# Attention heads on the whole array: zero-padded low query parts and meta tokens in place of 64- and 16-row products

## The chip, the cores and the metric

The kernel runs on one core of one Trainium2 chip. The metric is the device time of one execution in microseconds (us). TensorE multiplies (PE in the profile, its weight loads are PEld), VectorE (DVE), ScalarE (ACT) and GpSimd (POOL) do the elementwise work, and SyncE (SP) issues most DMAs. Each engine takes its own instructions in the order in which they were put into the program.

## The reference: what is computed

A trunk of two layers over 16 learned meta tokens and 512 input tokens (T = 528) of 1024 features. Layer 0 is a forgetting attention with 16 heads of 64 features, layer 1 a gated DeltaNet with 8 heads of 128; each is followed by a feed-forward part with a causal convolution. The change is in the attention alone, which is, for one head:

```python
q, k = rmsnorm(q, q_gain), rmsnorm(k, k_gain)
c = cumsum(log_sigmoid(fl + b_forget))
s = q @ k.T * 64 ** -0.5 + c[:, None] - c[None, :]
p = softmax(where(causal, s, -1e30))
o = (p @ v) * sigmoid(og)
```

All inputs and outputs are float32.

## The kernel before

**Tiling and stages.** Features lie on the partitions, tokens on the free axis. The tokens are worked on in two halves: A with 272 (16 meta tokens and 256 others) and B with 256. Weights come as units of 1024 input features by 128 output features. `dense` (L300 to L317) makes one unit's product for one half: eight feature tiles, and for each three matmuls at L312, since every float32 operand is split into a high and a low float32r part (high times high, high times low, low times high), so 24 matmuls of 128 x 128 weights over 256 or 272 columns. `push` (L425) runs half A of a unit at once and half B four units later.

**The attention stage** has 33 input units: one for the forget gates, then for each of eight pairs of heads (loop at L531) one for queries, keys, values and output gates. A pair's heads are e = 0 and e = 1, with 64 features each, so that a pair fills the 128 partitions.

- `qk` (L545 to L579) norms queries and keys. For keys it writes one tile `KS` per head: the high parts on that head's 64 partitions, the low parts on the other 64. For queries it writes per head a tile `QS` with the high parts on both halves of the partitions, and one tile `QL` for both heads, with the low parts of head e on head e's 64 partitions.
- `vproj` (L581 to L607) turns the values so that tokens lie on the partitions, and splits them: `VV` holds four blocks of 128 tokens, `VM` the 16 meta tokens on 16 partitions for each head (0 to 15 and 32 to 47).
- `attend` (L609 to L708) runs when a half's output gates are through `dense`. Its query blocks are `QB` (L490): block 0 is the 16 meta tokens, blocks 1 to 4 have 128 tokens. Half A takes blocks 0, 1 and 2, half B 3 and 4. `scores` (L624) makes for each head and block the product `QS` by `KS` (128 rows, L637), the product `QL` by the high keys on 64 rows (L638), and adds the causal mask as a bf16 product (L640); block 4 has its keys in two segments. DVE adds the decays (L641), ACT exponentiates (L644), DVE normalizes (L645, L646).
- `flip` (L651) transposes the probabilities on PE, a 128 x 128 block of keys at a time (L671), and splits them into `PTH` (ACT, L674) and `PTL` (DVE, L675). The first 32 keys, with the meta tokens, are transposed apart, 32 wide: those of head 0 to partitions 0 to 31 (L662), those of head 1 by a plain matmul with the identity to partitions 32 to 63 (L663, two passes). They become `PMH` and `PML` (L664, L665).
- `values` (L678) makes for each head and half the product of probabilities and values at L694: high and low probabilities over two (A) or four (B) blocks of 128 tokens, and for the meta tokens a product over 16 rows with `PMH` and one with `PML`.

**What sets the order.** The kernel is emitted unit by unit, and the framework puts each engine's instructions in an order at build time, by priorities and a simulated timeline (`schedule_with_timeline_sim=True`, L1470). So the heads' products lie between the `dense` products of the following units in PE's queue. The steps of `qk`, `vproj` and `og` behind `dense` have a raised priority (`tc.high_priority(offset=400)`).

**PSUM.** A tile is one bank. In the attention (L126) `dense` has two banks, `sc` (scores) two, `pt` (transposes) two, `av` and `pn` one each. `flip` takes one `pt` bank for block 0, two for blocks 1 to 3 and three for block 4; `vproj` takes one for each half.

**Weights.** ACT makes each unit's high part (L285), and for nearly all attention units GpSimd makes the low part in two instructions (L292). GpSimd also writes half of `QS` (L574), zeroes 16 columns of block 0's scores (L648) and does a step of the gates (L720).

Of the kernel before, what the change touches and what calls it, by code (L numbers as in the profile page):

```python
# [28 lines left out]
# estimated times (us) after which the DeltaNet's tasks go on  # L29
# [8 lines left out]
# order of the DeltaNet's units: queries, keys, values, output gates (H) and output projection, of head pairs  # L38
# [5 lines left out]
# units of the DeltaNet that leave work to GpSimd: low parts of weights, convolution taps, silu products  # L44
# [60 lines left out]
def trunk(ctx, tc, h0, wflat, params, out):  # L105
# [5 lines left out]
    # token range of the halves; the last layer leaves out the meta tokens but the two that its convolution sees  # L111
# [10 lines left out]
    # PSUM: one bank per tile; which ring of banks a kind of tile takes depends on the phase  # L122
# [48 lines left out]
    # constants  # L171
# [82 lines left out]
        # runs the tasks on, past their times, until a condition holds  # L254
# [15 lines left out]
    # weight stream  # L270
# [60 lines left out]
    # (mean of squares + eps) ** -0.5 per token, spread over the partitions in PSUM;  # L331
    # half A is covered by three chunks of 128 tokens, the last two of which overlap;
    # GpSimd adds the squares of the tiles
# [39 lines left out]
    # h * gain split in two float32r parts; the per-token factor is applied after the product  # L373
# [48 lines left out]
    # the job pipeline: half B of a unit runs LAG units behind half A  # L422
# [26 lines left out]
    # ---------------- output projections into m, then post-norm and next pre-norm  # L449
# [28 lines left out]
    # ---------------- FoX attention  # L478
# [13 lines left out]
    def attention_heads(layer, OH, OL, cx):  # L492
# [4 lines left out]

        def evac_f(u, half):
# [11 lines left out]
            # log_sigmoid(z) = min(z, 0) - log1p(exp(-|z|))  # L510
# [20 lines left out]
        for m in range(8):  # L531
            H = {}

            def head_tiles(m=m, H=H):
                if H:
                    return
                for e in range(2):
                    H["k", e] = ap.tile([P, T], F32R, name="KS", tag="KS", bufs=4)
                # values in two parts, [high, low] of head 0 and [low, high] of head 1
                H["v"] = ap.tile([P, 4, 2, 2, DH], F32R, name="VV", tag="VV", bufs=2)  # L540
                H["vm"] = ap.tile([48, 2, DH], F32R, name="VM", tag="VM", bufs=2)
                for half in range(2):
                    H["sg", half] = ap.tile([P, 272], F32, name="SG", tag="SG", bufs=4)

            def qk(u, half, which, H=H, m=m, head_tiles=head_tiles):  # L545
# [4 lines left out]
                with tc.high_priority(offset=400):  # L550
# [5 lines left out]
                    sx = ap.tile([P, 2, 272], F32R, name="SX", tag="SX", bufs=2)[:, :, :n]  # L556
                    nc.scalar.copy(sx[:, 0], sq)
                    nc.vector.tensor_tensor(sx[:, 1], sq, sx[:, 0].bitcast(F32), op=ALU.subtract)
                    nc.tensor.matmul(pn[:, :n], blk[:], sx[:, 0], start=True, stop=False)
                    nc.tensor.matmul(pn[:, :n], blk[:], sx[:, 1], start=False, stop=True)  # L560
                    # (mean of squares + eps) ** -0.5
# [3 lines left out]
                    if which == "q":  # L565
                        for e in range(2):
                            H["q", half, e] = ap.tile([P, 272], F32R, name="QS", tag="QS", bufs=4)
                        H["ql", half] = ap.tile([P, 272], F32R, name="QL", tag="QL", bufs=2)
                    for e in range(2):
                        a, b = (slice(0, 64), slice(64, 128)) if e == 0 else (slice(64, 128), slice(0, 64))  # L570
                        if which == "q":
                            S, L = H["q", half, e][:, :n], H["ql", half][:, :n]
# [8 lines left out]
            def vproj(u, half, H=H, m=m):  # L581
# [3 lines left out]
                with tc.high_priority(offset=400):  # L585
# [7 lines left out]
                    if half == 0:  # L593
                        nc.tensor.transpose(pt[:NM, 256:384], vr[:, 0:NM], ident[:])
                    b0 = blocks[0] - 1
                    VV, VM = H["v"], H["vm"]
                    sv = pt[:, 0:256].rearrange("p (k e x) -> p k e x", k=2, e=2)
                    for e in range(2):
                        vh, vl = VV[:, b0:b0 + 2, e, e, :], VV[:, b0:b0 + 2, e, 1 - e, :]
                        nc.scalar.copy(vh, sv[:, :, e, :])  # L600
                        nc.vector.tensor_tensor(vl, sv[:, :, e, :], vh.bitcast(F32), op=ALU.subtract)
                    if half == 0:
                        for e in range(2):
                            sv = pt[:NM, 256 + DH * e:256 + DH * e + DH]
                            o = slice(32 * e, 32 * e + NM)
                            nc.scalar.copy(VM[o, e, :], sv)
                            nc.vector.tensor_tensor(VM[o, 1 - e, :], sv, VM[o, e, :].bitcast(F32), op=ALU.subtract)  # L607

            def attend(half, H=H, m=m):  # L609
# [5 lines left out]
                PMH = ap.tile([64, 272], F32R, name="PMH", tag="PMH", bufs=2)  # L615
                PML = ap.tile([64, 272], F32R, name="PML", tag="PML", bufs=2)
# [7 lines left out]
                def scores(e, qb):  # L624
                    a = slice(0, 64) if e == 0 else slice(64, 128)
                    cB = Z[e][0]
                    QS, QL, KS = H["q", half, e], H["ql", half], H["k", e]
                    qs, ql = QB[qb]
                    ke = qs + ql
                    S = ap.tile([P, T], F32, name="S", tag="S", bufs=4)  # L630
                    st = ap.tile([P, 4], F32, name="st", tag="st", bufs=6)
                    segs = ((0, ke),) if ke <= 512 else ((0, 264), (264, 264))
                    for i, (k0, kn) in enumerate(segs):
                        sc = psum_tile("sc")
                        lastseg = k0 + kn == ke
                        o = sc[:ql, 0:kn]
                        nc.tensor.matmul(o, QS[:, qs - s:ke - s], KS[:, k0:k0 + kn], start=True, stop=False)  # L637
                        nc.tensor.matmul(o, QL[a, qs - s:ke - s], KS[a, k0:k0 + kn], start=False, stop=not lastseg)  # L638
                        if lastseg:
                            nc.tensor.matmul(sc[:ql, kn - ql:kn], identb[:ql, :ql], cmask[:ql, :ql], start=False, stop=True)  # L640
                        nc.vector.tensor_tensor_reduce(out=S[:ql, k0:k0 + kn], in0=o, in1=cB[:ql, k0:k0 + kn], scale=1.0, scalar=3e38, op0=ALU.add, op1=ALU.min, accum_out=st[:ql, i:i + 1])  # L641
                    if len(segs) == 2:
                        nc.vector.tensor_tensor(st[:ql, 0:1], st[:ql, 0:1], st[:ql, 1:2], op=ALU.min)
                    nc.scalar.activation(S[:ql, 0:ke], S[:ql, 0:ke], AF.Exp, scale=-1.0, bias=st[:ql, 0:1], accum_out=st[:ql, 2:3])  # L644
                    nc.vector.reciprocal(st[:ql, 3:4], st[:ql, 2:3])  # L645
                    nc.vector.tensor_scalar(S[:ql, 0:ke], S[:ql, 0:ke], st[:ql, 3:4], None, op0=ALU.mult)  # L646
                    if qb == 0:
                        nc.gpsimd.memset(S[:ql, 16:32], 0.0)  # L648
                    return S

                def flip(qb, SS):  # L651
                    qs, ql = QB[qb]
                    ke = qs + ql
# [821 lines left out]
```

## Time and profile before

| what | value |
|---|---|
| median of 3 runs | 1652.77 us (1651.1 to 1657.88) |
| span of the profiled execution | 1652.0 us |
| PE, PEld busy | 96%, 91% of the span |
| DVE, ACT, POOL busy | 68%, 49%, 30% |
| mean granted clock of TensorE | 0.978 |
| moved from and to HBM | 131.54 and 5.36 MB, 83 GB/s |

The profiled execution has no other time than its span, first to last instruction; it lies 0.8 us under the median of the runs. The input units of the attention run from about 5 us to about 393 us; then come its output projection and the first feed-forward part (to about 810 us), the DeltaNet (to about 1230 us) and the second feed-forward part. A matmul's duration in the profile (293 ns for a 128 x 256 one at L312) is longer than its share of PE's time, since matmuls overlap; the distance from one start to the next tells what a matmul costs, and the timeline shows that.

### The profile page before, as it was taken

Reading aid. Unit: us, or ns where it says so; the run is one execution under the profiler, and the core shown is the slowest. Engines: PE = TensorE matmul, PEld = TensorE weight load, DVE = VectorE, ACT = ScalarE, POOL = GpSimd, SP = SyncE. Lnnn points to the kernel's source line nnn. Section 1 sums busy time; section 2 is a strip of 40 time slices with the busy share of each in tenths; the row PEclk is TensorE's granted clock in tenths of the full one; section 3 lists DMA queues with packets and bytes.
Section 4 is the critical chain, followed back from the end, with each engine's and each line's share of the span. In section 5 each row is a group of like instructions: output and inputs, shape, how many; then the busy total and the mean of one; then the engine's idle time right before and its main releaser. Section 6 shows DMA issues by size and latency. Waiting matters only on the chain.

```text
span 1652.0 us, 33460 instructions
## 1 busy us (share of the span) xinstructions
PE 1588.7 (96%) x12702; PEld 1505.8 (91%) x12702; DVE 1128.9 (68%) x2652; ACT 817.3 (49%) x1949; POOL 490.5 (30%) x979
## 2 busy tenths in 40 slices
PE   8999999999999999999989899999997999999996
PEld 7888888888999999999978888898997999999996
DVE  7777777774897467566588765576559874675764
ACT  7666666663564344244455455545555543443441
POOL 6333333211530000001354763836235210100012
PEclk9999999999999999999989998989998999999998
DMA  5222222231222322322223323131232223323221
GB/s 169 85 72 66 58 66 72 72 117 59 83 90 81 95 94 81 99 90 90 81 84 100 91 70 75 44 98 44 63 117 84 90 84 96 103 79 101 90 78 52
DMA packets 63328, 139.05 MB, mean 84 GB/s; under 512 B 18584, under 2 KB 31288, under 8 KB 62784
## 3 DMA queue, kind: packets, MB, share of 16 engines
q1 hardware_dynamic: 62544, 134.55, 27.5%
q8 instruction: 100, 1.64, 0.4%
q0 software_dynamic: 480, 2.15, 0.4%
q14 instruction: 60, 0.49, 0.1%
q10 hardware_dynamic: 144, 0.22, 0.0%
HBM read 131.54 MB, written 5.36 MB: 83 GB/s over the span
## 4 chain that ended last, share of the span: by engine, by line
PE 76%; DVE 8%; POOL 7%; DMA 3%; ACT 2%; issue 2%; SPq 1%; POOLq 0%; DVEq 0%; ACTq 0%
PE ps L312 64%; PE av L694 3%; POOL PR L1172 3%; POOL RB L1173 3%; PE sc L638 2%; DVE cv L759 1%; DVE h L412 1%; DVE bt L411 1%; PE pt L671 1%; DMA w<-wflat 1%; PE sc L637 1%; DVE wl L292 1%; DMA AB<-dA 1%; DVE xl L378 1%; PE pt L663 1%
## 5 line engine op out<-in xcount | busy, mean ns | idle before, releaser
L312 PE MATMUL ps<-xh,wh 128*128 128x256 f32 (+4 forms) x2464 | 716.2, 293 | 19.1 <-DVE ub L743 10.9
L312 PE MATMUL ps<-xl,wh 128*128 128x256 f32 (+4 forms) x2464 | 710.9, 289 | 2.8 <-DVE xl L378 2.8
L312 PE MATMUL ps<-xh,wl 128*128 128x256 f32 (+4 forms) x2464 | 709.5, 289 | 0.0
L312 PEld LDWEIGHTS ps<-xh,wh 128*128 128x128 f32 (+1 forms) x2464 | 468.1, 191 | 28.2 <-DVE ub L743 8.1
L312 PEld LDWEIGHTS ps<-xl,wh 128*128 128x128 f32 (+1 forms) x2464 | 470.0, 191 | 7.0 <-DVE xl L378 3.9
L312 PEld LDWEIGHTS ps<-xh,wl 128*128 128x128 f32 (+1 forms) x2464 | 469.8, 191 | 1.3 <-issue 0.3
L285 ACT CAST wh<-w 128x1024 fp32r<-128x1024 f32 (+3 forms) x226 | 224.7, 996 | 190.3 <-PE ps L312 168.8
L292 DVE TENSOR_TENSOR wl<-w,wh 128x1024 fp32r<-128x1024 f32 (+4 forms) x191 | 221.7, 1161 | 101.1 <-ACT wh L285 100.5
L759 DVE SCALAR_TENSOR_TENSOR cv<-ub,prm,cv 128x256 f32<-128x256 f32 (+2 forms) x494 | 243.8, 498 | 40.7 <-ACT cv L750 31.6
L312 PE MATMUL ps<-ah,wl 128*128 128x256 f32 (+2 forms) x704 | 199.5, 284 | 0.0
L312 PE MATMUL ps<-ah,wh 128*128 128x256 f32 (+2 forms) x704 | 199.3, 283 | 0.0
L312 PE MATMUL ps<-al,wh 128*128 128x256 f32 (+2 forms) x704 | 199.1, 283 | 0.0
L750 ACT ACTIVATE cv<-ub,prm 128x256 f32<-128x256 f32 (+2 forms) x224 | 113.5, 509 | 144.8 <-DVE ub L743 144.6
L743 DVE TENSOR_TENSOR ub<-ps,r 128x256 f32<-128x256 f32 (+2 forms) x224 | 95.1, 427 | 93.9 <-PE ps L312 91.1
L312 PEld LDWEIGHTS ps<-ah,wh 128*128 128x128 f32 x704 | 132.7, 189 | 0.0
L312 PEld LDWEIGHTS ps<-al,wh 128*128 128x128 f32 x704 | 132.5, 188 | 0.0
L312 PEld LDWEIGHTS ps<-ah,wl 128*128 128x128 f32 x704 | 132.4, 188 | 0.0
L353 POOL TENSOR_TENSOR ssq<-ssq,sq 128x256 f32<-128x256 f32 (+2 forms) x98 | 89.3, 914 | 139.8 <-ACT sq L352 138.1
L292 POOL TENSOR_TENSOR wl<-w,wh 128x512 fp32r<-128x512 f32 x70 | 95.1, 1379 | 110.9 <-ACT wh L285 104.5
L746 POOL COPY cy<-ub 128x2 f32<-128x2 f32 (+1 forms) x112 | 38.5, 346 | 276.0 <-DVE ub L743 275.7
L742 POOL COPY ub<-cy 128x2 f32<-128x2 f32 (+1 forms) x112 | 32.1, 286 | 199.5 <-DVE cv L759 164.2
L1172 POOL TENSOR_TENSOR PR<-RB,AB 128x60 f32<-128x60 f32 (+24 forms) x124 | 50.6, 408 | 24.3 <-DMA AB<-dA 9.9
(310 smaller groups left out, 2481.6 us busy)
## 6 DMA issues: line engine op xcount, KB each, us to landing
w<-wflat SPq DMA_DIRECT2D x176, 512.0 KB, 3.6
w<-wflat SPq DMA_DIRECT2D x32, 448.0 KB, 3.3
cB<-cdram SPq DMA_DIRECT2D x16, 264.0 KB, 3.3
w<-wflat SPq DMA_DIRECT2D x16, 256.0 KB, 2.7
h<-h SPq DMA_DIRECT2D x8, 272.0 KB, 4.4
cB<-cdram SPq DMA_DIRECT2D x16, 136.0 KB, 3.1
h<-h SPq DMA_DIRECT2D x8, 256.0 KB, 5.6
AB<-dA SPq DMA_DIRECT2D x16, 128.0 KB, 2.8
```

Of the source, the lines that this page charges most:

```text
L285: nc.scalar.copy(wh[:], w32)
L292: eng.tensor_tensor(wl[:, c], w32[:, c], wh[:, c].bitcast(F32), op=ALU.subtract)
L312: tok(nc.tensor.matmul(o, w[:, a], r[:, c0:c1], start=(i == 0), stop=(i == tot - 1)))
L353: nc.gpsimd.tensor_tensor(self.acc[:, :n], self.acc[:, :n], sq[:, :n], op=ALU.add)
L638: nc.tensor.matmul(o, QL[a, qs - s:ke - s], KS[a, k0:k0 + kn], start=False, stop=not lastseg)
L694: nc.tensor.matmul(o, l, r, start=(i == 0), stop=(i == len(mm) - 1))
L743: nc.vector.tensor_tensor(ub[:, c0:c0 + n], ps, r[:, :n], op=ALU.mult)
L746: nc.gpsimd.tensor_copy(c[:, :c0], ub[:, n:n + c0])
L750: nc.scalar.activation(cv, ub[:, c0:c0 + n], AF.Identity, scale=w[c0])
L759: nc.vector.scalar_tensor_tensor(cv, ub[:, i:i + n], w[i], cv, op0=ALU.mult, op1=ALU.add)
L1172: nc.gpsimd.tensor_tensor(t, R3[:, 0:a, l:l + 1].to_broadcast([P, a, w]), A3[:, l:l + 1, l + 1:32].to_broadcast([P, a, w]), op=ALU.mult)
L1173: nc.gpsimd.tensor_tensor(R3[:, 0:a, l + 1:32], R3[:, 0:a, l + 1:32], t, op=ALU.subtract)
```

## The change

Every product of the heads gets 128 rows and 128 columns of weights:

- `QL` becomes one tile per head, with zeros on the other head's 64 partitions, so that L638's product runs over 128 rows. The tiles (`QZ`, two for each head) are made once, zeroed by GpSimd at the start of the stage, and taken in turn.
- Block 0's scores are made for 128 query rows, of which 16 are used; the mask product has 128 x 128 weights. GpSimd zeroes 112 columns of the scores on 128 partitions in place of 16 on 16.
- The first keys' probabilities are transposed as 128 x 128 blocks, one for each head, both by a transpose. One tile `PM` (again two, zeroed once) holds the high parts of the 16 meta rows on partitions 0 to 15 and their low parts on 32 to 47, zeros elsewhere, for both heads side by side on the free axis.
- The meta tokens' values become a fifth block of `VV`: GpSimd copies the first 32 tokens four times side by side, and one 128 x 128 transpose puts them on the partitions, so that rows 0 to 15 and 32 to 47 both hold the meta tokens. One product of 128 rows takes the place of the two of 16 rows in `values`.
- `vproj` splits the values with fewer, wider instructions: one on ACT and one on DVE for both heads, and one each for the meta block.
- `flip` takes the bank of the meta rows first: one bank for block 0, two for block 1 and three for blocks 2, 3 and 4.
- `SX` becomes `SH` (two buffers) and `SL` (one), and the gates' tile `SG` has two buffers in place of four and is taken in `og`.

The diff without the parts that only drop comments:

```diff
+        zt = bl[:, 0:1]
+        nc.vector.memset(zt, 0.0)
+        QZ = [[ap.tile([P, 272], F32R, name=f"QZ{i}{e}") for e in range(2)] for i in range(2)]
+        PZ = [ap.tile([P, 2, 272], F32R, name=f"PZ{i}") for i in range(2)]
+        for i in range(2):
+            for e in range(2):
+                b = slice(64, 128) if e == 0 else slice(0, 64)
+                nc.gpsimd.tensor_copy(QZ[i][e][b, :], zt[b, :].to_broadcast([64, 272]))
+            nc.gpsimd.tensor_copy(PZ[i][:], zt.unsqueeze(1).to_broadcast([P, 2, 272]))
+        ring = {"q": 0, "p": 0}
+
+        def persistent(name, tiles):
+            ring[name] += 1
+            return tiles[ring[name] % 2]
...
-                H["v"] = ap.tile([P, 4, 2, 2, DH], F32R, name="VV", tag="VV", bufs=2)
-                H["vm"] = ap.tile([48, 2, DH], F32R, name="VM", tag="VM", bufs=2)
-                for half in range(2):
-                    H["sg", half] = ap.tile([P, 272], F32, name="SG", tag="SG", bufs=4)
+                H["v"] = ap.tile([P, 5, 4, DH], F32R, name="VV", tag="VV", bufs=2)
...
-                    sx = ap.tile([P, 2, 272], F32R, name="SX", tag="SX", bufs=2)[:, :, :n]
+                    sh = ap.tile([P, 272], F32R, name="SH", tag="SH", bufs=2)[:, :n]
+                    sl = ap.tile([P, 272], F32R, name="SL", tag="SL", bufs=1)[:, :n]
...
-                        H["ql", half] = ap.tile([P, 272], F32R, name="QL", tag="QL", bufs=2)
+                        H["ql", half] = persistent("q", QZ)
...
-                        nc.tensor.transpose(pt[:NM, 256:384], vr[:, 0:NM], ident[:])
+                        vm = tmp2("vm")[:, 0:P]
+                        nc.gpsimd.tensor_copy(vm.rearrange("p (r x) -> p r x", r=4), vr[:, 0:32].unsqueeze(1).to_broadcast([P, 4, 32]))
+                        nc.tensor.transpose(pt[:, 256:384], vm, ident[:])
+                    VV = H["v"]
                     b0 = blocks[0] - 1
-                    VV, VM = H["v"], H["vm"]
-                    sv = pt[:, 0:256].rearrange("p (k e x) -> p k e x", k=2, e=2)
-                    for e in range(2):
-                        vh, vl = VV[:, b0:b0 + 2, e, e, :], VV[:, b0:b0 + 2, e, 1 - e, :]
-                        nc.scalar.copy(vh, sv[:, :, e, :])
-                        nc.vector.tensor_tensor(vl, sv[:, :, e, :], vh.bitcast(F32), op=ALU.subtract)
-                    if half == 0:
-                        for e in range(2):
-                            sv = pt[:NM, 256 + DH * e:256 + DH * e + DH]
-                            o = slice(32 * e, 32 * e + NM)
-                            nc.scalar.copy(VM[o, e, :], sv)
-                            nc.vector.tensor_tensor(VM[o, 1 - e, :], sv, VM[o, e, :].bitcast(F32), op=ALU.subtract)
+                    for k0, nb, sv in ((b0, 2, pt[:, 0:256]), (4, 1, pt[:, 256:384]))[:2 if half == 0 else 1]:
+                        sv = sv.rearrange("p (k e x) -> p k e x", k=nb, e=2)
+                        vh, vl = VV[:, k0:k0 + nb, 0:4:3, :], VV[:, k0:k0 + nb, 1:3, :]
+                        nc.scalar.copy(vh, sv)
+                        nc.vector.tensor_tensor(vl, sv, vh.bitcast(F32), op=ALU.subtract)
...
+                    qc = slice(qs - s, qs - s + P)
...
-                        nc.tensor.matmul(o, QS[:, qs - s:ke - s], KS[:, k0:k0 + kn], start=True, stop=False)
-                        nc.tensor.matmul(o, QL[a, qs - s:ke - s], KS[a, k0:k0 + kn], start=False, stop=not lastseg)
+                        nc.tensor.matmul(o, QS[:, qc], KS[:, k0:k0 + kn], start=True, stop=False)
+                        nc.tensor.matmul(o, QL[:, qc], KS[:, k0:k0 + kn], start=False, stop=not lastseg)
                         if lastseg:
-                            nc.tensor.matmul(sc[:ql, kn - ql:kn], identb[:ql, :ql], cmask[:ql, :ql], start=False, stop=True)
+                            nc.tensor.matmul(sc[:, kn - ql:kn], identb[:], cmask[:, :ql], start=False, stop=True)
...
-                        nc.gpsimd.memset(S[:ql, 16:32], 0.0)
+                        nc.gpsimd.memset(S[:, ke:P], 0.0)
...
+                    pm = psum_tile("pt")
+                    for e in range(2):
+                        nc.tensor.transpose(pm[:, e * P:e * P + P], SS[e][:, 0:P], ident[:])
+                    pv = pm[0:NM, 0:2 * P].rearrange("p (e q) -> p e q", e=2)[:, :, 0:ql]
+                    nc.scalar.copy(PM[0:NM, :, qc], pv)
+                    nc.vector.tensor_tensor(PM[32:32 + NM, :, qc], pv, PM[0:NM, :, qc].bitcast(F32), op=ALU.subtract)
+                    if qb == 0:
+                        return
...
-                            nc.tensor.transpose(pm[0:32, mc:mc + ql], SS[0][:ql, 0:32], ident[:ql, :ql])
-                            nc.tensor.matmul(pm[32:64, mc:mc + ql], SS[1][:ql, 0:32], ident[:ql, :ql], start=True, stop=True)
-                            nc.scalar.copy(PMH[:, qc], pm[0:64, mc:mc + ql])
-                            nc.vector.tensor_tensor(PML[:, qc], pm[0:64, mc:mc + ql], PMH[:, qc].bitcast(F32), op=ALU.subtract)
...
+                        pt = pm[:, 256:512] if qb == 1 and e == 0 else psum_tile("pt")
...
-                        o = slice(32 * e, 32 * e + NM)
-                        mm = []
-                        for pmx, ptx in ((PMH, PTH), (PML, PTL)):
-                            mm.append((av[:, 0:n], VM[o], pmx[o, 0:n]))
+                        mm = [(av[:, 0:n], VV[:, 4, 2 * e:2 * e + 2], PM[:, e, 0:n])]
+                        for ptx in (PTH, PTL):
                             for kb in range(1, nkb + 1):
                                 lo = max(QB[kb][0], q0h)
-                                mm.append((av[:, lo - s:n], VV[:, kb - 1, e], ptx[:, kb - 1, lo - q0h:256]))
+                                mm.append((av[:, lo - s:n], VV[:, kb - 1, 2 * e:2 * e + 2], ptx[:, kb - 1, lo - q0h:256]))
...
+                    H["sg", half] = ap.tile([P, 272], F32, name="SG", tag="SG", bufs=2)
                     sg = H["sg", half][:, :n]
```

More of the change, by code (lines that the diff above doesn't have):

```diff
@@ L555, in qk @@
                     pn = psum_tile("pn")
-                    sx = ap.tile([P, 2, 272], F32R, name="SX", tag="SX", bufs=2)[:, :, :n]
[L557 to L560, printed above, removed]
+                    sh = ap.tile([P, 272], F32R, name="SH", tag="SH", bufs=2)[:, :n]
+                    sl = ap.tile([P, 272], F32R, name="SL", tag="SL", bufs=1)[:, :n]
+                    nc.scalar.copy(sh, sq)
+                    nc.vector.tensor_tensor(sl, sq, sh.bitcast(F32), op=ALU.subtract)
+                    nc.tensor.matmul(pn[:, :n], blk[:], sh, start=True, stop=False)
+                    nc.tensor.matmul(pn[:, :n], blk[:], sl, start=False, stop=True)
                     nc.scalar.activation(sq, pn[:, :n], AF.Ln, bias=epst[:])
@@ L571, in qk @@
                         if which == "q":
-                            S, L = H["q", half, e][:, :n], H["ql", half][:, :n]
+                            S, L = H["q", half, e][:, :n], H["ql", half][e][:, :n]
                             nc.scalar.copy(S[a, :], qr[a, :])
@@ L614, in attend @@
                 Z = []
-                PMH = ap.tile([64, 272], F32R, name="PMH", tag="PMH", bufs=2)
-                PML = ap.tile([64, 272], F32R, name="PML", tag="PML", bufs=2)
+                PM = persistent("p", PZ)
                 for e in range(2):
@@ L624, in scores @@
                 def scores(e, qb):
-                    a = slice(0, 64) if e == 0 else slice(64, 128)
                     cB = Z[e][0]
-                    QS, QL, KS = H["q", half, e], H["ql", half], H["k", e]
+                    QS, QL, KS = H["q", half, e], H["ql", half][e], H["k", e]
                     qs, ql = QB[qb]
                     ke = qs + ql
+                    qc = slice(qs - s, qs - s + P)
                     S = ap.tile([P, T], F32, name="S", tag="S", bufs=4)
@@ L652, in flip @@
                     qs, ql = QB[qb]
-                    ke = qs + ql
-                    qc = slice(qs - s, ke - s)
-                    mc = qb * 128 if qb < 4 else 0
+                    qc = slice(qs - s, qs - s + ql)
+                    pm = psum_tile("pt")
[3 more added lines that the diff above has]
+                    nc.scalar.copy(PM[0:NM, :, qc], pv)
@@ L656, in flip @@
+                    nc.vector.tensor_tensor(PM[32:32 + NM, :, qc], pv, PM[0:NM, :, qc].bitcast(F32), op=ALU.subtract)
+                    if qb == 0:
+                        return
+                    x0 = qs - q0h
                     for e in range(2):
                         S = SS[e]
[L658 to L667 removed]
@@ L668, in flip @@
-                        if qb:
-                            PTH, PTL = Z[e][1:]
-                            for kb in range(1, qb + 1):
-                                nc.tensor.transpose(pt[:, (kb - 1) * 128:kb * 128], S[:, QB[kb][0]:QB[kb][0] + 128], ident[:])
-                            x0 = qs - q0h
-                            pv = pt[:, 0:qb * 128].rearrange("p (k q) -> p k q", q=128)
-                            nc.scalar.copy(PTH[:, 0:qb, x0:x0 + 128], pv)
-                            nc.vector.tensor_tensor(PTL[:, 0:qb, x0:x0 + 128], pv, PTH[:, 0:qb, x0:x0 + 128].bitcast(F32), op=ALU.subtract)
+                        pt = pm[:, 256:512] if qb == 1 and e == 0 else psum_tile("pt")
@@ new lines, in flip @@
+                        PTH, PTL = Z[e][1:]
+                        for kb in range(1, qb + 1):
+                            nc.tensor.transpose(pt[:, (kb - 1) * 128:kb * 128], S[:, QB[kb][0]:QB[kb][0] + 128], ident[:])
+                        pv = pt[:, 0:qb * 128].rearrange("p (k q) -> p k q", q=128)
+                        nc.scalar.copy(PTH[:, 0:qb, x0:x0 + 128], pv)
+                        nc.vector.tensor_tensor(PTL[:, 0:qb, x0:x0 + 128], pv, PTH[:, 0:qb, x0:x0 + 128].bitcast(F32), op=ALU.subtract)
```

20 lines of the change are left out of this document (7 added, 13 removed).

## The prediction

> **What bounds the kernel now.** I read the page first, its shares and its slices.
>
> ```profile
> PE 1588.7 (96%) x12702; PEld 1505.8 (91%) x12702; DVE 1128.9 (68%) x2652; ACT 817.3 (49%) x1949; POOL 490.5 (30%) x979
> PE   8999999999999999999989899999997999999996
> DVE  7777777774897467566588765576559874675764
> ```
>
> A slice is 41.3 us, so the attention (5 to 393 us) is the first nine and a half: PE at 9 tenths, DVE at 7. PE's 9 is not yet a proof, since overlapping matmuls count as busy even when slow. So second I asked who makes PE and its weight loads wait between 28 and 390 us.
>
> ```profile
> PE ps L312 <- DVE fc L526: 1.8, 1, 1.8
> PE sc L637 <- DVE KS L579: 0.2, 1, 0.2
> ...
> PEld pt L663 <- issue: 6.4, 31, 0.2
> ...
> PEld sc L638 <- issue: 3.1, 16, 0.2
> ```
>
> The first two rows are all of PE's own waits for others: 2.0 us in 362. What the weight loads show instead is idle time that nobody releases ("issue"), always 0.2 us long, and always ahead of small products: L663 has 32 weight columns, L638 has 64 rows. So PE is the bound of this stage, and some of its time goes at those products. Third, one pair of heads by its length (chain of waits, whose last column is the count) and its engines (windows; per engine busy us and instructions, then granted clock).
>
> ```profile
> 91.38 1.84 PE av L694 x10
> ...
> 179.80 1.84 PE av L694 x10
> ```
>
> ```profile
> 104.00:148.00 44.00, 43.90 (x307) 37.37 (x308) 31.27 (x96) 27.34 (x77) 15.41 (x17) 1.00 0.24 68
> ```
>
> The same products return after two pairs, so a pair takes 88.42 / 2 = 44.2 us. In it DVE is busy for 31.3, ACT 27.3, POOL 15.4, at full clock. There are eight pairs.
>
> **The price of products, from starts in PE's timeline.** Columns are start, duration, instruction. First the pace of whole-array work.
>
> ```profile
> 96.95 0.28 PE L312 MATMUL ps<-xh,wh 128*128 128x256 f32 x1
> ...
> 98.02 0.27 PE L671 MATMUL pt<-ident,S 128*128 128x128 f32 x1
> 98.05 0.36 PE L312 MATMUL ps<-xh,wl 128*128 128x256 f32 x1
> 98.25 0.28 PE L312 MATMUL ps<-xh,wh 128*128 128x256 f32 x1
> ```
>
> Nine 256-column products lie between 96.95 and 98.02: 0.119 us each, 0.126 at 272 columns in proportion. The whole transpose and the next product end at 98.25, so the transpose costs 98.25 - 0.119 - 98.02 = 0.11.
>
> *Scores* (272 keys):
>
> ```profile
> 88.06 0.28 PE L312 MATMUL ps<-xh,wh 128*128 128x256 f32 x1
> 88.18 0.29 PE L637 MATMUL sc<-KS,QS 128*128 128x272 f32 x1
> 88.40 0.39 PE L638 MATMUL sc<-KS,QL 64*128 64x272 f32 x1
> 88.72 0.23 PE L640 MATMUL sc<-cmask,identb 128*128 128x128 bf16 x1
> 88.76 0.36 PE L312 MATMUL ps<-xl,wh 128*128 128x256 f32 x1
> 88.96 0.28 PE L312 MATMUL ps<-xh,wl 128*128 128x256 f32 x1
> ```
>
> The whole product ahead of the 64-row one takes 0.22 in place of 0.126, the 64-row one 0.32. From 88.18 to 88.96 - 0.119 = 88.84 the three cost 0.66; the mask is 0.12 of it. After: 2 x 0.126 + 0.12 = 0.37. Saved: 0.29. There are 12 such groups in a pair (two heads; blocks 0 to 3 once, block 4 in two segments), 96 in all; 16 are block 0's, with 16 columns, where I have only bounds, 0 and 0.29, and take the middle: 80 x 0.29 + 16 x 0.15 = 25.6 us.
>
> *Flips of the first keys*:
>
> ```profile
> 99.68 0.28 PE L312 MATMUL ps<-xh,wl 128*128 128x256 f32 x1
> 99.80 0.27 PE L662 MATMUL pt<-ident,S 128*32 128x128 f32 x1
> 100.00 0.41 PE L663 MATMUL pt<-ident,S 128*32 128x128 f32 x2
> 100.34 0.39 PE L312 MATMUL ps<-xh,wh 128*128 128x256 f32 x1
> 100.56 0.28 PE L312 MATMUL ps<-xl,wh 128*128 128x256 f32 x1
> ```
>
> From 99.80 to 100.56 - 0.119 = 100.44: 0.64. After: two whole transposes, 0.22. Saved 0.42 in each of 32; the 8 of block 0 lie between 0 and 0.42, middle 0.21: 15.1 us. Here a rule speaks against the change: the Trainium skill ("TensorE: Matmul & The Clock Gate", LDWEIGHTS) says that a weight load takes its columns / 1.2 ns, so 128 columns load 80 ns longer than 32; by it the 80 transposes would give back up to 6.4 us where the load lies open, and the whole sum would be 63 us. The rows above say otherwise, with 0.20 for a 32-wide one and 0.11 for a whole one, and I keep 15.1.
>
> *Values* (half B, one head):
>
> ```profile
> 91.10 0.28 PE L312 MATMUL ps<-xh,wl 128*128 128x256 f32 x1
> 91.31 0.38 PE L694 MATMUL av<-PMH,VM 16*128 16x256 f32 x1
> 91.62 0.68 PE L694 MATMUL av<-PTHB,VV 128*128 128x256 f32 x4
> 92.23 0.38 PE L694 MATMUL av<-PML,VM 16*128 16x256 f32 x1
> 92.54 0.68 PE L694 MATMUL av<-PTLB,VV 128*128 128x256 f32 x4
> 93.06 0.28 PE L662 MATMUL pt<-ident,S 128*32 128x128 f32 x1
> ```
>
> From 91.10 + 0.119 = 91.22 to 93.06: 1.84. After: nine whole products, two of them over 128 columns, which I take at half: 7 x 0.119 + 2 x 0.06 = 0.95. Saved 0.89 per head; half A has the same two 16-row products and loses the same: 32 x 0.89 = 28.5 us. Some 0.1 of each may be counted twice with what follows, so the lower end is 25.
>
> Sum: 25.6 + 15.1 + 28.5 = 69.2 us, or 8.65 for a pair. Check from below: 192 `dense` products at 0.1225, 8 of the norms, 35 transposes at 0.11, 10 masks at 0.12, 24 score products of 227 columns on average (0.105) and 28 value products (3.4 at most) make 23.5 + 1.0 + 3.9 + 1.2 + 2.5 + 3.4 = 35.5 against 44.2: 8.7. I go with 69.
>
> **What it adds beside PE.** On DVE, per pair:
>
> ```profile
> L665 DVE TENSOR_TENSOR PML<-pt,PMH 64x128 fp32r<-64x128 f32 x16 | 4.4, 277 | 1.7 <-ACT PMH L664 1.5
> ...
> L601 DVE TENSOR_TENSOR VV<-pt,VV 128x128 fp32r<-128x128 f32 x16 | 4.2, 281 | 0.1
> ...
> L675 DVE TENSOR_TENSOR PTLA<-pt,PTHA 128x256 fp32r<-128x256 f32 x8 | 3.4, 423 | 1.5 <-ACT PTHA L674 1.4
> ...
> L607 DVE TENSOR_TENSOR VM<-pt,VM 16x64 fp32r<-16x64 f32 x8 | 1.7, 213 | 0.1
> ```
>
> Four low parts of `PM` grow from 128 columns to 256 (0.277 to 0.423): +0.58. The values' six (4 x 0.281 + 2 x 0.213) become two of 256 and one of 128 columns (1.13): -0.42. Net +0.2, so 31.5 us, 88% of a pair of 35.6. ACT makes the same trade. GpSimd's copies at the start (four of 64 x 272, two of 128 x 544) are bounded by its idle time there:
>
> ```profile
> 0.00:25.00 25.00, 19.97 (x121) 17.12 (x122) 19.56 (x41) 19.16 (x42) 15.45 (x25) 1.00 0.64 212
> ```
>
> It is idle for 9.5 us of the first 25. I take nothing; without that cover they would cost some us, once.
>
> New waits: the meta values now go through a GpSimd copy between DVE and PE, once a pair, behind what GpSimd has in its queue (rival two). Blocks 2 and 3 take a third `pt` bank, so two more times a pair a transpose can wait for ACT and DVE to empty a bank, with `dense` queued behind it on PE; I price it with the general loss: PE's waits go from zero now to the 2.3 us a pair of rival one, and I take the middle, 1.1 a pair, 9 us. `SG` with two buffers and `SL` with one are each rewritten a unit or more after their last reader; nothing.
>
> So 69 - 9 = 60 us: 1652.0 - 60 = 1592.0 for the profiled execution, which lies 0.8 below the median: 1592.8. All later stages only move ahead.
>
> **The rivals.**
> *One, DVE becomes the bound.* Its queue is also idle for ACT's sake, which a faster PE need not shorten. From the waits between 60 and 370 us:
>
> ```profile
> DVE st L645 <- ACT S L644: 10.1, 14, 0.9
> ...
> DVE wl L292 <- ACT wh L285: 2.1, 2, 1.6
> ```
>
> The nine groups from the first to the last of these in which DVE waits for ACT sum to 45 us in seven pairs, 6.4 a pair. A pair of 31.5 + 6.4 = 37.9 saves 6.3 x 8 = 50: 1602; with DVE's waits for PE not gone either, 39 a pair, 1611. For it: the 88%. Against: ACT's waits for PE cause part of those. Chance 0.25.
>
> *Two, slower: PE waits for GpSimd's copy of the meta values.* GpSimd often stands at the head of a weight's low part:
>
> ```profile
> POOL wl L292 <- ACT wh L285: 98.6, 18, 10.7
> ```
>
> If the copy is queued behind that wait, and the transpose stands in PE's queue, all of PE stands: 5.5 us on average, 10.7 at worst, once a pair. At worst 1652.8 - 69 + 8 x 10.7 = 1669, at the average 1628. It turns slower than before from 8.6 us a pair. Against: the other GpSimd results that PE needs, `QS` and the zeroed scores, end none of PE's waits above. Chance 0.03, half of it slower.
>
> *Three, the small products ran beside others.* If so, padding takes real PE time: 96 score products at 0.105, 32 of the meta values at 0.1225 and 80 transposes at 0.11 would be added, 23 us: 1676. The Trainium skill says this in "TensorEngine Tiling (Array Packing)", When to Use Tiling: a contract dimension of 64 or less calls for row tiling, up to twice as fast. Here the trace disagrees: the product after a 64-row one starts 0.32 us later, not sooner. Chance 0.02.
>
> *Four, nothing*: PE's freed time turns to waits throughout, 1652. The 2.0 us of waits speak against it. Chance 0.03.
>
> **How the numbers follow.** The forecast, 1592.8, has 0.67, and its own range goes from 1580 (no new waits, block 0 saving fully) to 1602 (all of rival one's loss). The range for 8 in 10 reaches from 1578 to 1616, over rival one's worse end. Half a per cent, 8 us, is about what a measurement can tell. Faster: 0.67 + 0.25 + 0.01 of rival two = 0.93; same 0.03; slower 0.02 + 0.02 = 0.04.
>
> **What would show it.** Right: a pair of 36 to 37.5 us; L638 and its neighbours starting 0.12 to 0.13 apart at 272 columns; two transposes in 0.22 us; a value group of 0.95 us; the "issue" waits ahead of L663, L638 and L694 gone; DVE near 31.5 us a pair; the later stages as long as before. Wrong: PE waiting for DVE or ACT by more than 2.3 us a pair (rival one), PE's transposes of the values waiting for POOL (two), or slots of padded products longer than those of `dense` (three).

## The result and the profile after

The changed kernel takes 1605.09 us (median of 4 executions, 1601.35 to 1605.29) against 1652.41 us for the kernel before: a ratio of 0.9694, 95% interval 0.9672 to 0.9717. Its profiled execution has a span of 1599.4 us, at a mean clock of 0.977; the three others had clocks of 0.971 to 0.973 and spans of 1603 us. So the profile, whose clock is that of the profile of before (0.978), shows the larger gain: 52.6 us.

From the page of the changed kernel, the shares and slices again:

```profile
PE 1525.8 (95%) x12630; PEld 1486.8 (93%) x12630; DVE 1123.4 (70%) x2629; ACT 815.4 (51%) x1925; POOL 495.8 (31%) x993
PE   8999999999999999999789899899989999999996
DVE  7888888948974675674978665676569864765764
```

The attention is now 8.4 slices of 40.0 us, and in it DVE stands at 8 tenths where it stood at 7. The chain of waits shows where the stage ends; the first two rows are of the kernel before, the last of the changed one (start, us, what, count):

```profile
386.34 1.85 PE av L694 x10
...
389.77 1.86 PE av L694 x10
```

```profile
338.24 1.01 PE av L698 x9
```

The last values are through at 391.6 and at 339.3 us: 52.4 of the 52.6 us are gained in the attention. The length of a pair comes from the meta product of half A (272 columns, first head), which starts at 148.44 and four pairs later at 325.31 us before, at 133.25 and 282.84 after: 44.2 and 37.4 us. One pair of the changed kernel in the windows, and who made PE (and, in the last row, its weight loads) wait between 94 and 282 us, which is five pairs:

```profile
169.74:207.37 37.63, 36.38 (x300) 35.23 (x298) 31.20 (x95) 27.40 (x76) 15.47 (x18) 1.00 0.28 79
```

```profile
PE pt L678 <- DVE PZ L669: 2.6, 4, 0.7
PE sc L646 <- DVE st L650: 2.2, 4, 0.6
...
PEld L649 <- issue: 1.5, 9, 0.2
```

PE now is idle for 37.63 - 36.38 = 1.25 us of this pair, and in the five pairs for 4.8 us on account of DVE, 1.0 a pair; DVE is busy for 31.2, as before, but of 37.6 us. The "issue" waits of the weight loads ahead of the low score products, the first keys' transposes and the value products are gone; those ahead of the bf16 masks (L649) stay. The new prices are in PE's timeline:

```profile
190.28 0.28 PE L646 MATMUL sc<-KS,QS 128*128 128x272 f32 x1
190.40 0.29 PE L647 MATMUL sc<-KS,QZ 128*128 128x272 f32 x1
190.53 0.23 PE L649 MATMUL sc<-cmask,identb 128*128 128x128 bf16 x1
190.57 0.37 PE L312 MATMUL ps<-xh,wl 128*128 128x272 f32 x1
190.78 0.60 PE L678 MATMUL pt<-ident,S 128*128 128x128 f32 x4
...
192.46 0.40 PE L666 MATMUL pt<-ident,S 128*128 128x128 f32 x2
192.62 0.36 PE L312 MATMUL ps<-xh,wh 128*128 128x256 f32 x1
192.82 0.28 PE L312 MATMUL ps<-xl,wh 128*128 128x256 f32 x1
...
196.20 0.36 PE L312 MATMUL ps<-xh,wl 128*128 128x256 f32 x1
196.41 0.28 PE L698 MATMUL av<-PZ,VV 128*128 128x256 f32 x1
196.52 0.57 PE L698 MATMUL av<-PTHB,VV 128*128 128x256 f32 x4
196.94 0.63 PE L698 MATMUL av<-PTLB,VV 128*128 128x256 f32 x4
197.40 0.29 PE L678 MATMUL pt<-ident,S 128*128 128x128 f32 x1
```

A score group goes from 190.28 to 190.78 less one `dense` product (0.126), that is 0.37 us (forecast 0.37); a flip of the first keys from 192.46 to 192.82 - 0.119, 0.24 us (0.22); a value group of half B from 196.41 to 197.40, 0.99 us (0.95).

### The profile page after: what moved, and what is told of

Its sections match the earlier page's. It is cut to its first block, busy times and chain, and to the rows that moved or that the text cites. A ratio compares the mean times of both kernels' runs of the same rounds, so it can differ in the third digit from the quotient of the medians.

```text
span 1599.4 us, 33295 instructions
## 1 busy us (share of the span) xinstructions
PE 1525.8 (95%) x12630; PEld 1486.8 (93%) x12630; DVE 1123.4 (70%) x2629; ACT 815.4 (51%) x1925; POOL 495.8 (31%) x993
## 4 chain that ended last, share of the span: by engine, by line
PE 74%; DVE 11%; POOL 5%; DMA 4%; ACT 3%; issue 3%; SPq 1%; POOLq 0%; DVEq 0%; ACTq 0%
PE ps L312 65%; POOL PR L1177 2%; POOL RB L1178 2%; DVE h L412 1%; DVE bt L411 1%; DVE wl L292 1%; PE av L698 1%; DMA w<-wflat 1%; DVE cv L764 1%; DMA gcr<-gcd 1%; PE pt L678 1%; DVE xl L378 1%; ACT wh L285 1%; PE s L1277 1%; DVE qr L577 1%
## 5 line engine op out<-in xcount | busy, mean ns | idle before, releaser
L312 PE MATMUL ps<-xh,wh 128*128 128x256 f32 (+4 forms) x2464 | 717.6, 293 | 16.8 <-DVE ub L748 9.2
L312 PE MATMUL ps<-xl,wh 128*128 128x256 f32 (+4 forms) x2464 | 710.8, 289 | 3.4 <-DVE xl L378 3.0
L312 PE MATMUL ps<-xh,wl 128*128 128x256 f32 (+4 forms) x2464 | 713.6, 290 | 0.0
L312 PEld LDWEIGHTS ps<-xh,wh 128*128 128x128 f32 (+1 forms) x2464 | 469.6, 192 | 22.8 <-DVE ub L748 6.3
L312 PEld LDWEIGHTS ps<-xl,wh 128*128 128x128 f32 (+1 forms) x2464 | 471.1, 191 | 7.4 <-DVE xl L378 4.6
L312 PEld LDWEIGHTS ps<-xh,wl 128*128 128x128 f32 (+1 forms) x2464 | 471.1, 191 | 1.0
L764 DVE SCALAR_TENSOR_TENSOR cv<-ub,prm,cv 128x256 f32<-128x256 f32 (+2 forms) x494 | 243.8, 498 | 38.4 <-ACT cv L755 29.5
L312 PE MATMUL ps<-ah,wl 128*128 128x256 f32 (+2 forms) x704 | 199.5, 284 | 0.0
L312 PE MATMUL ps<-ah,wh 128*128 128x256 f32 (+2 forms) x704 | 199.3, 283 | 0.0
L312 PE MATMUL ps<-al,wh 128*128 128x256 f32 (+2 forms) x704 | 199.1, 283 | 0.0
L312 PEld LDWEIGHTS ps<-ah,wh 128*128 128x128 f32 x704 | 132.6, 189 | 0.0
L312 PEld LDWEIGHTS ps<-al,wh 128*128 128x128 f32 x704 | 132.5, 188 | 0.0
L312 PEld LDWEIGHTS ps<-ah,wl 128*128 128x128 f32 x704 | 132.4, 188 | 0.0
L786 ACT ACTIVATE gl<-cv 128x272 f32<-128x272 f32 (+2 forms) x88 | 36.7, 418 | 42.0 <-DVE cv L764 41.7
```

The costliest lines, as they stand in the source:

```text
L312: tok(nc.tensor.matmul(o, w[:, a], r[:, c0:c1], start=(i == 0), stop=(i == tot - 1)))
L764: nc.vector.scalar_tensor_tensor(cv, ub[:, i:i + n], w[i], cv, op0=ALU.mult, op1=ALU.add)
L786: nc.scalar.activation(g, cv, AF.Gelu_apprx_tanh)
```

## The experiments

Two theories were named on record. **S**: what the change takes away is the switch between whole-array products and small ones, once in and once out for each stretch; PE is still the bound, and its waits for DVE are the small rest. **D**: DVE is the bound of the changed kernel. Later experiments ask for the price itself: **P** says that each small product has it, not each stretch. Every edit is to the changed kernel; "slower" is against it, and its ratio to the kernel before is 0.9694. A pair is measured as above, over four pairs of the profiled execution unless said.

### Undoing one part at a time

**u_scores**, the low query parts on 64 rows:

```diff
-                        nc.tensor.matmul(o, QL[:, qc], KS[:, k0:k0 + kn], start=False, stop=not lastseg)
+                        nc.tensor.matmul(o, QL[64 * e:64 * e + 64, qc], KS[64 * e:64 * e + 64, k0:k0 + kn], start=False, stop=not lastseg)
```

> The changed kernel with the low query parts' product back on 64 rows (same order of instructions on PE and DVE). Theory S (what the change saves is the switch to and from small products, PE is still the bound, and the prices of the trace of before hold): 96 groups at 0.29 us less for block 0's, so 23 to 28 us slower than the changed kernel. Rival D (DVE is now the bound, and PE has 1.2 to 1.5 us a pair to spare): the first 10 to 12 us are hidden, so 12 to 17 us slower.

Measured: 1627.93 us, ratio 0.9828 (0.9777 to 0.9879), 22 us over the changed kernel by the ratios. The pair grows from 37.4 to 39.9 us, 2.5 or 20 us in all. In PE's timeline the group has its old price:

```profile
201.42 0.28 PE L646 MATMUL sc<-KS,QS 128*128 128x272 f32 x1
201.63 0.39 PE L647 MATMUL sc<-KS,QZ 64*128 64x272 f32 x1
201.95 0.23 PE L649 MATMUL sc<-cmask,identb 128*128 128x128 bf16 x1
201.99 0.37 PE L312 MATMUL ps<-xh,wl 128*128 128x272 f32 x1
202.20 0.60 PE L678 MATMUL pt<-ident,S 128*128 128x128 f32 x4
```

From 201.42 to 202.20 - 0.126 it is 0.65 us; before the change it was 0.66, in the changed kernel 0.37. The 20 us lie between the two theories: the price is that of S, but part of it falls into PE's waits for DVE, which go down from 4.8 us between 94 and 282 us to 2.6.

**u_flips**, the first keys' transposes 32 wide:

```diff
-                        nc.tensor.transpose(pm[:, e * P:e * P + P], SS[e][:, 0:P], ident[:])
+                        nc.tensor.transpose(pm[0:32, e * P:e * P + P], SS[e][:, 0:32], ident[:])
```

> The changed kernel with the first keys' transposes 32 columns wide again, both heads by a transpose. Theory S: 0.20 us each and 0.1 us for the way back, against 0.11 each: 0.28 us in each of 40 flips, 9 to 12 us slower than the changed kernel. Rival D: hidden up to 1.2 to 1.5 us a pair, so 0 to 2 us slower. By the page's rule that a load takes its columns / 1.2 ns, 6 us faster.

Measured: 1605.3 us, ratio 0.9696 (0.9658 to 0.9733), a pair of 37.4 us: nothing. Theory S misses, and so does the rule on weight loads that the prediction took from the Trainium skill ("TensorE: Matmul & The Clock Gate", LDWEIGHTS), by which the run would have been 6 us faster. A flip of two 32-wide transposes in its timeline:

```profile
193.07 0.38 PE L666 MATMUL pt<-ident,S 128*32 128x128 f32 x2
193.20 0.36 PE L312 MATMUL ps<-xh,wh 128*128 128x256 f32 x1
193.40 0.28 PE L312 MATMUL ps<-xl,wh 128*128 128x256 f32 x1
```

From 193.07 to 193.40 - 0.119 it takes 0.21 us, as whole ones do. So the width of a transpose is no part of the price, and the price of the old flips is still to be found (below).

**u_values64**, the meta values' product on the 64 rows that are not all zero:

```diff
-                        mm = [(av[:, 0:n], VV[:, 4, 2 * e:2 * e + 2], PM[:, e, 0:n])]
+                        mm = [(av[:, 0:n], VV[0:64, 4, 2 * e:2 * e + 2], PM[0:64, e, 0:n])]
```

> The changed kernel with the one product of the meta values over 64 rows in place of 128 (the rest are zeros either way; same order on PE and DVE, as many products). Theory S: one way in (0.1 us) and one way out (0.19 us) for each of 32, 8 to 10 us slower than the changed kernel. Rival P (the price is that of the number of small products, not of the switch, since the change also halved their number): 0 us. Rival D: 0 us, hidden in 1.2 to 1.5 us a pair.

Measured: 1611.75 us, ratio 0.9728 (0.9695 to 0.9762); a pair of 38.4 us, 1.0 more, 8 us in all. By the ratios it is 6 us, and their intervals overlap a little, so the pairs and the timeline decide.

```profile
200.31 0.36 PE L312 MATMUL ps<-xh,wl 128*128 128x256 f32 x1
200.60 0.38 PE L698 MATMUL av<-PZ,VV 64*128 64x256 f32 x1
200.91 0.68 PE L698 MATMUL av<-PTHB,VV 128*128 128x256 f32 x4
201.43 0.64 PE L698 MATMUL av<-PTLB,VV 128*128 128x256 f32 x4
```

Beside the rows of the changed kernel: the product ahead takes 0.29 us in place of 0.21, the small one 0.31 in place of 0.11, the four behind it 0.52 in place of 0.42. The number of products and their order are the same; only the rows differ. S's 8 to 10 us are just reached by the pairs, and D's nothing falls: PE's time still counts. The Trainium skill names a mechanism ("TensorEngine Tiling (Array Packing)", Tiling Modes): changing the tiling mode drains the engine. The late starts on both sides agree with it, but no run here shows the drain itself. It gives no price; here it is about 0.1 us in and 0.2 to 0.3 out.

### Stretch or product, and whether two small products run side by side

**p_whole** and **p_rows** put both heads' score products next to each other in PE's queue; they have the same order on PE and differ in the rows of the low products alone:

```diff
+                        for e in range(2):
+                            tc.stamp_issue_order_token(nc.tensor.matmul(sc[e][:, 0:kn], H["q", half, e][:, qc], H["k", e][:, k0:k0 + kn], start=True, stop=False).ins, "sc")
+                        for e in range(2):
+                            a = slice(64 * e, 64 * e + 64)
+                            tc.stamp_issue_order_token(nc.tensor.matmul(sc[e][:, 0:kn], H["ql", half][e][a, qc], H["k", e][a, k0:k0 + kn], start=False, stop=not lastseg).ins, "sc")
```

(p_whole has `:` in place of both `a`; the masks follow for both heads in the same way.)

> The changed kernel with the score products of a pair's two heads put side by side in PE's queue (both heads' high products, then both low ones, then both masks), all on 128 rows. It is the base for the next run. Both theories: within 10 us of the changed kernel; the order costs something where the second head's bank is late.

> As the run before, with the two low products on 64 rows each, head 0 on rows 0 to 63, head 1 on 64 to 127, next to each other in PE's queue, into two banks; otherwise the same order. Theory S (the price is one way in and one way out, 0.1 + 0.19 us, for each stretch of small products): 48 stretches in place of 96, so 12 to 14 us slower than the run before, 6 us less if the two run at the same time. Rival P (each small product has the price): 23 to 28 us slower, as when they stood alone. By the page's rule for row tiling (twice as fast): 6 us faster.

Measured: p_whole 1610.93 us, ratio 0.9737 (0.9695 to 0.9778), a pair of 37.7; p_rows 1619.5 us, ratio 0.9787 (0.9754 to 0.9819). The clock of p_rows dipped (0.96 from 132 to 170 us); the two pairs at full clock after that are 38.4 us, against 38.0 and 37.9 of p_whole. By the pairs that is 3.4 us in all, by the medians 9, against 6 to 8 for S with two products at a time, 12 to 14 for S without, and 23 to 28 for P. The intervals overlap, so the price is read from the timeline, p_whole first:

```profile
217.65 0.41 PE L644 MATMUL sc<-KS,QS 128*128 128x264 f32 x2
217.89 0.41 PE L647 MATMUL sc<-KS,QZ 128*128 128x264 f32 x2
218.13 0.29 PE L312 MATMUL ps<-xh,wh 128*128 128x272 f32 x1
218.26 0.29 PE L312 MATMUL ps<-xl,wh 128*128 128x272 f32 x1
```

```profile
221.27 0.40 PE L644 MATMUL sc<-KS,QS 128*128 128x264 f32 x2
221.60 0.39 PE L647 MATMUL sc<-KS,QZ 64*128 64x264 f32 x2
221.92 0.39 PE L312 MATMUL ps<-xh,wh 128*128 128x272 f32 x1
222.15 0.29 PE L312 MATMUL ps<-xl,wh 128*128 128x272 f32 x1
```

Less one `dense` product, the four take 0.48 us whole (217.65 to 218.26) and 0.75 in rows (221.27 to 222.15): 0.27 for the two small ones together, where u_scores pays 0.28 for each. This is the dearest stretch of its pair. Where the masks follow directly, the difference is 0.17 (184.23 to 184.72 whole, 187.71 to 188.37 in rows) or less. That, and waits of PE for DVE that shrink by about 0.4 us a pair, is why the pair grows so little. P falls. And the two 64-row products together start the next one after 0.32 us, as a single one did in u_scores: they do run at the same time, on the two halves of the rows, as the Trainium skill has it ("TensorEngine Tiling (Array Packing)", Tiling Modes: different tiles can load and multiply in parallel). What that wins is less than the way in and out costs: side by side is still dearer than whole.

### What made the old flips dear

**f_plain** and **f_column**: head 1's first keys by a plain product with the identity, as before the change, to partitions 0 to 31 or to 32 to 63, and the meta rows copied head by head. **f_whole**: the plain product 128 columns wide.

```diff
-                    for e in range(2):
-                        nc.tensor.transpose(pm[:, e * P:e * P + P], SS[e][:, 0:P], ident[:])
+                    nc.tensor.transpose(pm[0:32, 0:P], SS[0][:, 0:32], ident[:])
+                    nc.tensor.matmul(pm[0:32, P:2 * P], SS[1][:, 0:32], ident[:], start=True, stop=True)
```

In f_column the output is `pm[32:64, P:2 * P]`, in f_whole it is `pm[:, P:2 * P]` and the input `SS[1][:, 0:P]`.

> The changed kernel with head 1's first keys flipped by a plain float32 product with the identity, 32 columns wide, in two passes, as before the change, but to partitions 0 to 31, and the meta rows copied by two instructions per engine and flip in place of one. Since 32-wide transposes turned out to cost no more than whole ones, two theories are left for the 0.42 us of a flip. Theory F (the plain product's two passes): 0.3 to 0.4 us in each of 40 flips, 10 to 16 us slower than the changed kernel. Theory C (its output columns 32 to 63, a column tile): 0 to 4 us slower, from the copies alone.

> As the run before, with the plain product's output on partitions 32 to 63. Theory F: as slow as the run before. Theory C: 10 to 16 us slower than the run before.

> As the run with the plain 32-wide product to partitions 0 to 31, but the plain product 128 columns wide (same copies, same order on DVE). Theory F1 (the two float32 passes are the price): as slow as that run, a pair within 0.3 us of its 40.7. Theory F2 (the price is the switch of a plain product to 32 columns and back; the passes cost 0.1 us more than a transpose): 0.3 us less in each of 5 flips, so 1.3 to 1.6 us a pair and 10 to 13 us faster than that run.

Measured: f_plain 1632.9 us (ratio 0.9875, 0.9842 to 0.9909), f_column 1630.83 (0.9856, 0.9827 to 0.9886), f_whole 1626.66 (0.9833, 0.9793 to 0.9873). The output's place makes no difference, so C falls: f_plain has the whole price already. (PE's order differs between these two runs, but a flip in f_column's timeline, from the transpose's start at 194.13 to 194.90 less one `dense` product and 0.11 for the transpose, has 0.53 us for the two passes, as f_plain below.) f_plain is slower than F said, by 28 us in place of 10 to 16. First f_plain, then f_whole:

```profile
192.12 0.29 PE L312 MATMUL ps<-xh,wh 128*128 128x272 f32 x1
192.33 0.41 PE L666 MATMUL pt<-ident,S 128*32 128x128 f32 x2
192.67 0.39 PE L312 MATMUL ps<-xl,wh 128*128 128x272 f32 x1
192.90 0.29 PE L312 MATMUL ps<-xh,wl 128*128 128x272 f32 x1
```

```profile
207.74 0.29 PE L312 MATMUL ps<-xl,wh 128*128 128x272 f32 x1
207.87 0.38 PE L666 MATMUL pt<-ident,S 128*128 128x128 f32 x2
208.00 0.37 PE L312 MATMUL ps<-xh,wl 128*128 128x272 f32 x1
208.21 0.29 PE L312 MATMUL ps<-xh,wh 128*128 128x272 f32 x1
```

The two passes (x2) take 192.90 - 192.12 - 2 x 0.126 = 0.53 us at 32 columns and 208.21 - 207.74 - 2 x 0.126 = 0.22 at 128. So a plain float32 product of 128 columns costs 0.1 us more than a transpose, and 0.31 more again when it is 32 wide: F2's price. The 32-wide product is late on both sides like the 64-row ones: 0.21 us from the start of the product ahead, 0.34 for the two passes and 0.23 for the product behind, against 0.13, 0.13 and 0.21 when it is whole. That this is the same switch, for columns, is my reading; the runs show that the width of the plain product has the price. It takes a plain product to show it, since the 32-wide transposes of u_flips paid nothing.

The pair fell by only 0.7 us from f_plain to f_whole (40.6 to 39.9), not by the 1.3 to 1.6 expected, and f_whole is still 2.5 us a pair over the changed kernel, of which its plain products explain 0.5. The rest came with the copies by head: between 95 and 284 us PE's waits for DVE are 7.9 us in f_plain and 11.6 in f_whole, against 4.8 in the changed kernel. No run has these copies with whole transposes, so their own cost is not shown apart. The price of the old flips is therefore the one read from the timeline, not the 28 us.

### Is DVE the bound now?

**dve_relief** moves low parts of keys and output from DVE to GpSimd, **dve_double** makes them twice on DVE, **bank** changes when a `pt` bank is taken, **dve_bank** is dve_relief with bank.

```diff
-                            nc.vector.tensor_tensor(S[b, :], qr[a, :], S[a, :].bitcast(F32), op=ALU.subtract)
+                            nc.gpsimd.tensor_tensor(S[b, :], qr[a, :], S[a, :].bitcast(F32), op=ALU.subtract)
...
-                    nc.vector.tensor_tensor(ol, t[:, :n], oh.bitcast(F32), op=ALU.subtract)
+                    nc.gpsimd.tensor_tensor(ol, t[:, :n], oh.bitcast(F32), op=ALU.subtract)
...
-                        pt = pm[:, 256:512] if qb == 1 and e == 0 else psum_tile("pt")
+                        pt = pm[:, 256:512] if qb in (1, 2) and e == 0 else psum_tile("pt")
```

> The changed kernel with the low parts of the keys and of the output moved from DVE to GpSimd, 2.6 us a pair off DVE's queue. Theory S: at most PE's waits for DVE go, 1.2 us a pair, so 0 to 10 us faster than the changed kernel, or slower where GpSimd is late. Rival D: DVE's 2.6 us a pair show until PE is the bound again, 10 to 12 us faster.

> The changed kernel with DVE's low parts of the keys and of the output each made twice, 2.6 us a pair more on DVE's queue (about 34 of 37.4 us busy). Theory S: PE stays the bound with some more waits, 0 to 8 us slower than the changed kernel. Rival D: 2.6 us a pair, 19 to 22 us slower.

> The changed kernel with head 0's transposes of block 2 in the bank of the meta rows, as block 1's are: one bank less of the transposes' ring per pair. Theory S: PE's wait of 0.7 us a pair for the meta rows' bank goes, 0 to 6 us faster than the changed kernel. Rival D: no change, DVE sets the pair.

> Both at once: the low parts of the keys and of the output on GpSimd, and head 0's block 2 in the bank of the meta rows. Theory S: PE's remaining waits of 1.1 us a pair go for the greater part, 2 to 9 us faster than the changed kernel, with a pair of 36.3 to 37.1 us. Rival D: the pair falls with DVE's load, to 36 or less.

| run | us | ratio, interval | pair, us |
|---|---|---|---|
| dve_relief | 1602.81 | 0.9672, 0.9641 to 0.9704 | 37.1 |
| dve_double | 1626.64 | 0.9842, 0.9796 to 0.9888 | 40.3 |
| bank | 1610.42 | 0.974, 0.971 to 0.977 | 37.3 |
| dve_bank | 1604.25 | 0.9699, 0.9666 to 0.9732 | 37.6 |

dve_relief takes 2.6 us a pair off DVE's queue and gains 0.3 us a pair, inside the interval. DVE's busy time fell by less than was moved, from 31.2 to 30.3 us a pair, since other DVE instructions became longer (the 256-column `SL` at L571 went from 776 to 1069 ns); why stays open. All the same PE's waits for DVE between 94 and 282 us went from 4.8 to 0.4 us, with 1.4 us for GpSimd in their place, and the pair is hardly shorter. That is against D, which wanted 10 to 12 us, if less sharply than the edit was meant to ask.

But adding 2.6 us costs as much as D said: 22 us by the medians. The clock of dve_double dipped in the attention (0.97 from 94 to 282 us). One such dip is short: in steps of 4 us the clock is 1.00, 0.57 and 1.00 from 140 to 152 us, and PE was busy for only 2.5 of the first 4 us. So a dip may itself come from PE's waits, which is not shown further. Its pair at full clock, from 181.43 to 220.47 us, takes 39.0 us, 1.4 more than the same pair of the changed kernel, which is 11 us for eight. PE then waits for DVE at more places:

```profile
PE sc L647 <- DVE KS L593: 3.8, 4, 1.2
PE av L699 <- DVE avt L701: 2.0, 3, 1.4
PE sc L647 <- DVE st L651: 1.9, 3, 0.8
```

So S, which gave 0 to 8 us, misses as well. PE is the bound, and DVE is so close behind that added work there shows for the greater part. bank misses too, where S had 0 to 6 us to gain: its pair is 37.3. All queues were planned anew for it; PE waits less for the meta rows' bank between 94 and 282 us (1.3 us in place of 2.6), but more elsewhere, and its waits for DVE are 4.8 us in all as before. Its first pair is 40.1 us where the changed kernel's is 36.9, and there the granted clock was 0.96 (1.00 in the changed kernel), which is about 1.6 of the 3.2 us by an estimate (0.04 of 40.1); the rest stays open. dve_bank, with 37.6 against an expected 36.3 to 37.1, misses by both theories. No variant is clearly faster than the changed kernel.

## Why the prediction came out as it did

**The bound and the mechanism were right.** The gain lies in the attention alone, later stages kept their length, and small products among whole ones were the cost. What u_scores and u_values64 add, with nothing else changed, is 20 and 8 us. The fewer, wider instructions of `vproj` and the new use of banks and buffers were not undone one by one, so their share is not shown. One reading of the trace of before was too narrow: "issue" waits of the weight loads stood not only ahead of small products but also ahead of `dense` products at L312 (3.8 us, 19 times) and of the masks at L640 (3.1 us, 16 times). The masks stand right behind the 64-row products.

**The terms.** Score groups: forecast 0.29 saved, measured 0.66 - 0.37. Value groups of half B: forecast 0.89 with the way in, measured 1.84 - 0.99 = 0.85. Flips: forecast 0.42, measured 0.40, but its reason was wrong. I read 0.20 for a 32-wide transpose and took it for the price of its width; it was the way into the narrow plain product behind it, as u_flips, f_plain and f_whole show. The rule of the Trainium skill on loads ("TensorE: Matmul & The Clock Gate", LDWEIGHTS), which would have taken back 6 us, had nothing to show either: the loads of 32-wide transposes took 95 ns and those of whole ones 140, 45 ns more in place of 80, and the time was the same.

**The sum was a little too large.** I priced 8.65 us a pair for PE; it is 44.2 less 37.4, and the 1.0 to 1.25 us that PE now waits, so 7.8 to 8.0. Some of the 0.7 us that lacks is in half A's value groups, which I had priced like those of half B. From PE's timeline, one of before and one after, each from its first product to the transpose behind its last:

```profile
107.36 0.39 PE L694 MATMUL av<-PMH,VM 16*128 16x272 f32 x1
...
108.66 0.40 PE L592 MATMUL pt<-ident,vr 128*128 128x128 f32 x2
```

```profile
173.75 0.39 PE L698 MATMUL av<-PZ,VV 128*128 128x272 f32 x1
...
174.39 0.40 PE L605 MATMUL pt<-ident,vr 128*128 128x128 f32 x2
```

1.30 became 0.64, which with 0.1 for the way in is 0.76 saved in place of 0.89, twice a pair: 0.26. The flips lack 0.02 five times and half B's values 0.04 twice. The remaining 0.3 us a pair I can't put to a row.

**The loss to waits was right in size**: forecast 1.1 us a pair, measured 1.0 to 1.25, at one place that I had named (a bank of the transposes) and one that I had not (a bank of the scores).

**Rival one** comes close in number: a pair of 37.9 was its forecast, 37.4 the result, and its 1602 us lie nearer to the measured 1605.09 than the 1592.8 of the forecast. The forecast's own range ended at 1602 as well; only the wider one, to 1616, holds the median. As a mechanism it is half right: more DVE work costs time, less of it brings next to none. PE's waits of 1.0 to 1.25 us a pair stay under the 2.3 that was named as its sign. **Rival two** did not happen: no wait of PE for GpSimd's copy or the transposes behind it appears. **Rival three** has a true part, small products side by side do overlap, and the wrong sign. **Rival four** fell.

The forecast of 1592.8 us is 12 us under the median. Of that, 7 us are the profile's own (1599.4 against 1592.0), from the terms above; 1 lies around the span (the profiled execution took 1601.35), and 4 lie between it and the median, whose executions had the lower clock of 0.971 to 0.973.

## What to carry to other kernels

A product on part of the array that stands alone between whole-array products costs two switches, about 0.3 us here (32-wide transposes did not), and zero rows cost nothing next to that: pad it, or put small products next to each other. Look for it in starts, not in durations: the product ahead of a small one and the one behind it are both late. Once such time is out of a bound engine, ask who is next: here DVE took back 1 us of the 8 a pair.

## What was not expected of the hardware

- A transpose of float32 data 32 columns wide did not pay the switch (0.21 us for two in u_flips, against 0.24 for whole ones), a plain float32 product of the same width did (0.53 us in f_plain against 0.22 in f_whole).
- Two 64-row products on the two halves of the rows, into two banks, took as long as one (0.32 us to the next start in p_rows, as in u_scores).
- Executions of one kernel differ with their mean granted clock: u_scores took 1620.84 us at 0.978 and 1636.69 us at 0.964. Effects of a few us are therefore read from pairs at full clock, or from the timeline.
